# Moving TensorE's operands to whole kilobytes of a partition

## The chip, the cores and the metric

The kernel runs on one core of a Trainium2 chip. The metric is the device time of one execution in microseconds. A profile of one execution is read beside it: it gives the start and duration of each instruction on TensorE (PE for the matmuls, PEld for the loads of their stationary operand), VectorE (DVE), ScalarE (ACT), GpSimd (POOL), and the DMA transfers that SyncE (SP) issues.

## The reference

A decoder trunk of two layers over 256 tokens of width 2048. Layer 0 mixes tokens with 8 stick-breaking heads and 8 dilated-window heads, layer 1 with 16 forgetting-attention heads; each layer then has a gated MLP of inner width 5632 with a depthwise convolution of width 3, and a gated per-layer embedding:

```python
def reference(x, p, positions, ...):
    h = x
    for i in range(DEPTH):
        a = rmsnorm(h, attn_norm[i])
        if i % 2 == 0:
            h = h + sb_dilated_mixer(a, positions, w_in_even[i // 2], w_out_even[i // 2])
        else:
            h = h + fox_mixer(a, w_in_odd[i // 2], b_forget[i // 2], w_out_odd[i // 2])
        h = h + conv_ffn(rmsnorm(h, ffn_norm[i]), w_up[i], conv_w[i], conv_b[i], w_down[i])
        gate = jax.nn.sigmoid(rmsnorm(h, ple_norm[i]) @ w_ple_gate[i])
        h = h + gate * (p[i] @ w_ple[i])
    return rmsnorm(h, final_norm)
```

Everything is float32. Nearly all of the arithmetic is products of a 256-row activation with a weight matrix.

## The kernel before, in words

Activations lie transposed: the 2048 features are 16 tiles (`KT`) of 128 partitions, the 256 tokens run along the free dimension. A float32 product is made from three one-pass products of type float32r. Each operand is kept as two parts, a rounded value and the rest, and `PARTS` (line 194) lists which parts are multiplied: high by high, high by low, low by high.

The activations are in two buffers, `act0` and `act1` (line 114), which a layer uses in turn. One holds, for each of 16 feature tiles, the high part and the low part, 256 float32r each: 1 KB, 1 KB, and so on, 32 KB of each partition. `pact` (line 115) is the same for the per-layer input.

The weights come from memory in one stream in the order in which they are used (`UNITS`). `issue_group` loads up to 2048 columns into one of three `wr` buffers. `split_unit` (lines 158 to 168) makes the two parts of a unit, mostly four feature tiles by 256 output columns: ScalarE casts the high part into a `w` buffer (line 165), VectorE subtracts for the low part (line 166). There are four `w` buffers of 8 KB, and `unit` keeps three units split ahead of use.

`gemm_unit` (line 196) uses a unit in 24 matmuls at line 203. The stationary operand is 128 columns of `w` (512 bytes of each partition), the moving operand is one part of one feature tile of the activation, 256 columns, 1 KB. `gemm_v` (line 229) turns this round: at line 237 the activation is stationary and 256 columns of `w` are moving. `gemm_vf` (line 242) does so for 272 columns once. Each matmul is preceded by its own load of weights.

The program is written in one order; each engine takes its instructions in that order. The head-by-head work of the mixers is put off by a count of units (`defer`, `tick`), so that it falls between the units of the next products. There, score and attention matmuls take full float32 operands; the profile has two records for such a matmul, its two passes. The stick-breaking sums (lines 450 to 455) are again float32r, one pass, up to 512 columns wide.

Scratch tiles of 2 KB come from the tag `t2`, of which there are seven buffers. It serves the squares of the norms (`sq`), the two halves of an MLP group (`yg`, `yv`), the gate (`gt`) and some small tables.

Where a buffer lies within a partition follows from the order in which the pools are opened and the tiles are made. Ahead of all pools lie 16 KB that are set aside and 128 bytes of constants. So in the kernel before `h` begins 128 bytes past a whole kilobyte, and so does everything of whole kilobytes behind it; small tables in `cpool` then shift the weight pool, which begins 192 bytes past one.

Of the kernel before, what the change touches and what calls it, by code (L numbers as in the profile page):

```python
# [10 lines left out]
F32 = mybir.dt.float32  # L11
F32R = mybir.dt.float32r
# [5 lines left out]
P = 128  # L18
D = 2048
S = 256  # L20
# [5 lines left out]
KT = D // P  # L26
# [78 lines left out]
def trunk(ctx: ExitStack, tc: tile.TileContext, xT, pT, pos, gains, conv, bf, cst, wst, out):  # L105
    nc = tc.nc

    cpool = ctx.enter_context(tc.tile_pool(name="cpool", bufs=1))
    wpool = ctx.enter_context(tc.tile_pool(name="wpool", bufs=1))
    work = ctx.enter_context(tc.tile_pool(name="work", bufs=1))  # L110
    psum = ctx.enter_context(tc.tile_pool(name="psum", bufs=1, space=bass.MemoryType.PSUM))

    h = cpool.tile([P, KT, S], F32, name="h")
    bufs = [cpool.tile([P, KT, 2, S], F32R, name=f"act{i}") for i in range(2)]
    pact = cpool.tile([P, 2, 2, S], F32R, name="pact")
    pl = cpool.tile([P, KT, S], F32, name="pl")
    gn = cpool.tile([P, 7, KT], F32, name="gn")
    cv = cpool.tile([P, DEPTH, 2 * FT, 4], F32, name="cv")
# [13 lines left out]
        return psum.tile([P, 2, 512], F32, name=name, tag="at", bufs=2)  # L132

    def t2_tile(name, shape=(P, 2, S), dt=F32):
        return work.tile(list(shape), dt, name=name, tag="t2", bufs=7)

    def t3_tile(name, shape=(P, 768), dt=F32):
        return work.tile(list(shape), dt, name=name, tag="t3", bufs=4)
# [136 lines left out]
    def norm_squares(op):  # L275
        hs = h[:, 2 * op:2 * op + 2, :]
        if op == 0:
            nc.scalar.activation(out=acc, in_=hs, func=AF.Square)
        else:
            sq = t2_tile("sq")  # L280
            nc.scalar.activation(out=sq, in_=hs, func=AF.Square)
            nc.vector.tensor_add(out=acc, in0=acc, in1=sq)
# [26 lines left out]
    def norm_rows(mixer):  # L309

        dg = t2_tile("nd", (P, 2, P))
        ps = at_tile("rps")
        for t in range(2):
            nc.vector.tensor_scalar_mul(out=dg[:, t, :], in0=ident, scalar1=rT[:, t:t + 1])
            if mixer is None:
                nc.tensor.matmul(ps[:, 0, t * P:(t + 1) * P], lhsT=ones, rhs=dg[:, t, :],
                                 start=t == 0, stop=True, skip_group_check=True)
        if mixer is None:
            return ps[:, 0, :S]
        dh, dl = t2_tile("ndh", (P, 2, P), F32R), t2_tile("ndl", (P, 2, P), F32R)  # L320
        nc.scalar.copy(out=dh, in_=dg)
        nc.vector.tensor_sub(out=dl, in0=dg, in1=dh.bitcast(F32))
        for i, x in enumerate((dh, dl)):
            nc.tensor.matmul(ps[:, 0, :S], lhsT=trir[:, 0, :], rhs=x, start=i == 0, stop=i == 1)
        nc.vector.tensor_copy(out=rb, in_=ps[:, 0, :S])
        if mixer:
            nc.vector.tensor_scalar_mul(out=rq, in0=rb, scalar1=SCALE)
# [490 lines left out]
```

## Time and profile before

| what | value |
|---|---|
| time, three runs | 2437.23 us median (2437.09 to 2437.77) |
| the profiled execution | 2438.14 us, of which its span is 2436.3 us |
| granted TensorE clock, mean over the span | 0.997 |
| PE busy | 2414.1 us, 99% of the span, 20990 matmul records |
| DVE busy | 1595.7 us, 65% |
| ACT busy | 1228.3 us, 50% |
| DMA | 458.06 MB, mean 188 GB/s |

The profile's durations of matmuls overlap, since a matmul begins while the one before it drains. The pace of TensorE is therefore read from starts: the time that a row of the chain of waits gives for so many matmuls, divided by their number. The chain of waits is the chain of work that ended last, in order of time. A group's row gives, behind the bar, the busy time of the group in us and the mean duration of one instruction in ns.

### The profile page before, as it was taken

What the parts mean: (1) busy time and instruction counts of PE and PEld (TensorE: products, weight loads), DVE (VectorE), ACT (ScalarE), POOL (GpSimd) and SP (SyncE); (2) the same over time, 40 slices, a digit from 0 to 9 for tenths busy, and PEclk for the clock granted to TensorE, in tenths of its full rate; (3) what the DMA queues carried; (4) which work ended last, traced back from release to release, by engine and by line L of the source; (5) the groups of instructions that cost most, each with busy time, mean ns of one, the idle gap of its engine ahead of it and who ended that gap; (6) DMA issues with size and microseconds to landing.
All of it is one profiled execution on the core that took longest, in us unless ns stands there. A gap on an engine that the chain in (4) does not pass through costs nothing.

```text
span 2436.3 us, 48002 instructions
## 1 busy us (share of the span) xinstructions
PE 2414.1 (99%) x20990; PEld 2400.5 (99%) x20990; DVE 1595.7 (65%) x2157; ACT 1228.3 (50%) x1548; POOL 2.5 (0%) x8
## 2 busy tenths in 40 slices
PE   8999999999999999999999999999999999999997
PEld 8999999999999999999999999999999999999997
DVE  7557666776567657767765555677765776567676
ACT  6554455555355445555554444555543554455553
POOL 0000000000000000000000000000000000000000
PEclk9999999999999999999999999999999999999998
DMA  7444445555555555555554444555555555555553
GB/s 268 169 177 173 169 177 191 194 197 198 190 191 192 188 208 190 191 185 203 187 184 170 165 169 165 190 191 192 195 198 194 191 192 189 203 195 186 189 198 120
DMA packets 66483, 458.06 MB, mean 188 GB/s; under 512 B 7408, under 2 KB 7424, under 8 KB 16608
## 3 DMA queue, kind: packets, MB, share of 16 engines
q1 hardware_dynamic: 66096, 454.53, 52.8%
q8 instruction: 164, 2.69, 0.4%
q0 software_dynamic: 176, 0.46, 0.1%
q14 instruction: 47, 0.39, 0.0%
HBM read 452.86 MB, written 2.10 MB: 187 GB/s over the span
## 4 chain that ended last, share of the span: by engine, by line
PE 97%; DVE 1%; DMA 1%; ACT 1%; issue 0%; SPq 0%; DVEq 0%; ACTq 0%
PE psu L203 39%; PE psd L203 20%; PE pso L203 7%; PE psk L203 7%; PE psv L237 7%; PE psq L203 7%; PE psg L203 7%; DMA wr<-in_w 1%; PE avp L520 1%; PE psp L203 0%; PE pse L716 0%; PE scs L469 0%; PE psv L250 0%; PE sps L511 0%; PE avp L522 0%; PE scs L467 0%
## 5 line engine op out<-in xcount | busy, mean ns | idle before, releaser
L166 DVE TENSOR_TENSOR w<-wr,w 128x1024 fp32r<-128x1024 f32 (+2 forms) x882 | 1051.4, 1193 | 701.2 <-ACT w L165 695.5
L165 ACT CAST w<-wr 128x1024 fp32r<-128x1024 f32 (+2 forms) x882 | 905.6, 1028 | 1082.5 <-PE psu L203 355.1
L203 PE MATMUL psu<-act,w 128*128 128x256 f32 x8448 | 959.3, 276 | 0.0
L203 PEld LDWEIGHTS psu<-act,w 128*128 128x128 f32 x8448 | 958.3, 188 | 0.0
L203 PE MATMUL psd<-act,w 128*128 128x256 f32 x4224 | 479.7, 276 | 0.0
L203 PEld LDWEIGHTS psd<-act,w 128*128 128x128 f32 x4224 | 479.2, 188 | 0.0
L203 PE MATMUL psq<-act,w 128*128 128x256 f32 x1536 | 185.2, 279 | 1.2 <-DVE w L166 1.0
L203 PEld LDWEIGHTS psq<-act,w 128*128 128x128 f32 x1536 | 179.8, 188 | 2.1 <-DVE w L166 1.5
L203 PE MATMUL psk<-act,w 128*128 128x256 f32 x1536 | 180.0, 277 | 0.0
L203 PEld LDWEIGHTS psk<-act,w 128*128 128x128 f32 x1536 | 176.7, 188 | 0.0
L203 PE MATMUL pso<-act,w 128*128 128x256 f32 x1536 | 175.8, 277 | 0.0
L203 PEld LDWEIGHTS pso<-act,w 128*128 128x128 f32 x1536 | 174.9, 188 | 0.0
L237 PE MATMUL psv<-w,act 128*128 128x256 f32 x1440 | 172.7, 279 | 0.0
L237 PEld LDWEIGHTS psv<-w,act 128*128 128x128 f32 x1440 | 168.4, 188 | 1.1
L203 PE MATMUL psg<-act,w 128*128 128x256 f32 x1440 | 164.4, 276 | 0.0
L203 PEld LDWEIGHTS psg<-act,w 128*128 128x128 f32 x1440 | 163.7, 188 | 0.0
L616 DVE TENSOR_TENSOR u<-psu,rb 128x512 f32<-128x512 f32 x88 | 60.8, 691 | 33.3 <-PE psu L203 33.2
L622 DVE SCALAR_TENSOR_TENSOR yg<-u,cv,yg 128x256 f32<-128x256 f32 x176 | 73.3, 477 | 0.0
L622 DVE SCALAR_TENSOR_TENSOR yv<-u,cv,yv 128x256 f32<-128x256 f32 x176 | 73.3, 477 | 0.0
L619 ACT ACTIVATE yg<-u,cv 128x256 f32<-128x256 f32 x88 | 48.0, 594 | 1.0 <-DVE u L616 1.0
L619 ACT ACTIVATE yv<-u,cv 128x256 f32<-128x256 f32 x88 | 48.0, 593 | 0.0
L261 ACT CAST act<-yg 128x512 fp32r<-128x512 f32 x44 | 27.3, 621 | 39.1 <-DVE yg L632 39.1
(173 smaller groups left out, 886.5 us busy)
## 6 DMA issues: line engine op xcount, KB each, us to landing
wr<-in_w SPq DMA_DIRECT2D x388, 1024.0 KB, 4.8
wr<-in_w SPq DMA_DIRECT2D x36, 768.0 KB, 4.3
wr<-in_w SPq DMA_DIRECT2D x8, 896.0 KB, 4.6
wr<-in_w SPq DMA_DIRECT2D x7, 512.0 KB, 6.9
h<-in_x SPq DMA_DIRECT2D x4, 512.0 KB, 7.1
out_dram<-h SPq DMA_DIRECT2D x8, 256.0 KB, 2.4
wr<-in_w SPq DMA_DIRECT2D x2, 816.0 KB, 4.6
ct<-in_c SPq DMA_DIRECT2D x1, 841.0 KB, 6.6
```

The lines of the kernel that those rows point to most:

```text
L165: nc.scalar.copy(out=w[:, :, 0, :], in_=raw)
L166: nc.vector.tensor_sub(out=w[:, :, 1, :], in0=raw, in1=w[:, :, 0, :].bitcast(F32))
L203: nc.tensor.matmul(ps[:, j, :], lhsT=w[:, k, s, js], rhs=act[:, k0 - koff + k, t, :], start=first and j + k + n == 0, stop=last and k == k ...
L237: nc.tensor.matmul(ps[:, t], lhsT=act[:, 4 * i + k, a, tsl], rhs=w[:, k, b], start=i + t + k + n == 0, stop=i == 3 and k == kc - 1 and n = ...
L261: nc.scalar.copy(out=dst[:, :, 0, :], in_=src)
L520: nc.tensor.matmul(av[:, 0, j * S:(j + 1) * S], lhsT=v[:, 0, js], rhs=w[:, j * S:(j + 1) * S], start=j == 0, stop=False, skip_group_check= ...
L616: nc.vector.tensor_mul(out=u[:, :, 2:], in0=ps, in1=rb2)
L619: nc.scalar.activation(out=y[:, j, :], in_=u[:, j, 2:], func=AF.Identity, bias=cv[:, l, t, 3:4], scale=cv[:, l, t, 2:3])
L622: nc.vector.scalar_tensor_tensor(out=y[:, j, :], in0=u[:, j, tap:tap + S], scalar=cv[:, l, t, tap:tap + 1], in1=y[:, j, :], op0=ALU.mult, ...
```

## The change

Two pools are opened first, `apool` and then `wpool`. `apool` begins with a tile `head` of 224 float32 that nothing uses; it fills 896 bytes, so that with the constants ahead of it a whole kilobyte is full. Behind it come `act0`, `act1` and `pact`, then the weight buffers; `h`, the tables and the scratch follow. To make room, the tag `t2` has six buffers rather than seven.

```diff
+    apool = ctx.enter_context(tc.tile_pool(name="apool", bufs=1))
+    wpool = ctx.enter_context(tc.tile_pool(name="wpool", bufs=1))
     cpool = ctx.enter_context(tc.tile_pool(name="cpool", bufs=1))
-    wpool = ctx.enter_context(tc.tile_pool(name="wpool", bufs=1))
...
+    apool.tile([P, 224], F32, name="head")
+    bufs = [apool.tile([P, KT, 2, S], F32R, name=f"act{i}") for i in range(2)]
+    pact = apool.tile([P, 2, 2, S], F32R, name="pact")
     h = cpool.tile([P, KT, S], F32, name="h")
-    bufs = [cpool.tile([P, KT, 2, S], F32R, name=f"act{i}") for i in range(2)]
-    pact = cpool.tile([P, 2, 2, S], F32R, name="pact")
...
     def t2_tile(name, shape=(P, 2, S), dt=F32):
-        return work.tile(list(shape), dt, name=name, tag="t2", bufs=7)
+        return work.tile(list(shape), dt, name=name, tag="t2", bufs=6)
```

Where the operands begin, in the two built programs:

| buffer | before | after |
|---|---|---|
| `act0`, `act1`, `pact` | 128 bytes past a KB | at a KB |
| `wr`, `w` | 192 bytes past a KB | at a KB |
| 1 KB moving operand, line 203 | bytes 128 to 1152: crosses one KB boundary | bytes 0 to 1024: crosses none |
| 1 KB moving operand, line 237 | bytes 192 to 1216: crosses one | bytes 0 to 1024: crosses none |
| 512-byte stationary operand, line 203 | 192 to 704, or 704 to 1216, which crosses | 0 to 512, or 512 to 1024: none crosses |
| 272-column moving operand (1088 bytes), line 250 | crosses one | crosses one |
| 512-column moving operand, line 450 | from 288: crosses two | from 160: crosses two |

No engine's instructions change their order. Of waits, those that a buffer fewer of `t2` brings are new. The place where one stands on a compute engine is the first norm, where ScalarE squares `h` into seven scratch tiles `sq` between its casts of weights (line 165 before, 168 after). Before:

```order
L281 ACTIVATE sq<-h 128x512 x2
L165 CAST w<-wr 128x4x256 [waits DMAHW5_49,DVE_49]
L281 ACTIVATE sq<-h 128x512 x2
L165 CAST w<-wr 128x4x256 [waits DMAHW6_49,DVE_49]
L281 ACTIVATE sq<-h 128x512 x3
L165 CAST w<-wr 128x4x256 [waits DMAHW7_49,DVE_49,PE_49]
```

With the change:

```order
L284 ACTIVATE sq<-h 128x512 x2
L168 CAST w<-wr 128x4x256 [waits DMAHW5_49,DVE_49]
L284 ACTIVATE sq<-h 128x512 x2
L168 CAST w<-wr 128x4x256 [waits DMAHW6_49,DVE_49]
L284 ACTIVATE sq<-h 128x512 x2
L284 ACTIVATE sq<-h 128x512 [waits DVE_49]
L168 CAST w<-wr 128x4x256 [waits DMAHW7_49,PE_49]
```

The seventh square now waits on VectorE, which must first have added the first square to `acc`; the cast behind it no longer needs a wait on VectorE of its own. The other new wait is one of the load of `pr` for layer 1, on SP's queue, on a matmul of the first norm.

## The prediction

> **What bounds the kernel now.** I read the page first, for the engine that never rests, then the chain of waits in order of time, for the pace of that engine.
>
> ```profile
> PE 2414.1 (99%) x20990; PEld 2400.5 (99%) x20990; DVE 1595.7 (65%) x2157; ACT 1228.3 (50%) x1548; POOL 2.5 (0%) x8
> PE 97%; DVE 1%; DMA 1%; ACT 1%; issue 0%; SPq 0%; DVEq 0%; ACTq 0%
> ```
>
> TensorE is 97% of the chain that ended last, so the time is a number of matmuls times the pace at which they start, plus little. The chain of waits gives the pace:
>
> ```profile
> 60.20 8.48 PE psq L203 x72
> 194.89 8.16 PE psv L237 x72
> 420.21 160.50 PE psu L203 x1416
> 580.71 87.04 PE psd L203 x768
> 1212.64 6.73 PE psv L250 x54
> ```
>
> In the MLP, 160.50 us for 1416 matmuls is 113.35 ns from start to start, 87.04 for 768 is 113.33. With the operands' roles turned round (line 237), 8.16/72 is 113.3 as well. I call this the clean pace. In some stretches of layer 0's mixer the same matmul starts every 8.48/72 = 117.8 ns: a second, slower pace, mostly behind full-float32 score matmuls. The 272-column ones start every 6.73/54 = 124.6 ns.
>
> Is 113.3 a wait on somebody? These are four stretches of 1.36 us in the MLP; the columns are each engine's busy time with its instructions, then granted clock, DMA share and GB/s:
>
> ```profile
> 667.75:669.11 1.36, 1.36 (x15) 1.36 (x14) 0.92 (x2) 1.05 (x1) 0.00 (x0) 1.00 0.72 301
> 669.11:670.47 1.36, 1.36 (x15) 1.36 (x14) 0.99 (x1) 0.00 (x0) 0.00 (x0) 1.00 0.00 0
> 670.47:671.83 1.36, 1.36 (x15) 1.36 (x14) 0.23 (x1) 1.05 (x1) 0.00 (x0) 1.00 0.71 96
> 671.83:673.19 1.36, 1.36 (x15) 1.36 (x14) 0.99 (x1) 0.00 (x0) 0.00 (x0) 1.00 0.88 373
> ```
>
> TensorE makes as many starts with no byte of DMA moving and ScalarE idle as at 373 GB/s, at full clock. So the pace is TensorE's own, and no other engine has to be made faster.
>
> **What a stream costs by itself.** The change can only act on the pace, so I ask what 113.3 consists of. Durations by form, full float32 first (two passes, each taking two steps per column), then the one-pass sums of line 450 to 452:
>
> ```profile
> L520 PE MATMUL avp<-s,v 128*128 128x256 f32 x48 | 14.3, 379 | 0.0
> L522 PE MATMUL avp<-s,v 128*128 128x128 f32 x48 | 9.2, 274 | 0.0
> L450 PE MATMUL sps<-el,trir 128*128 128x512 f32 x4 | 1.6, 392 | 0.0
> L452 PE MATMUL sps<-el,trir 128*128 128x256 f32 x4 | 1.1, 280 | 0.0
> ```
>
> In full float32, 128 more columns, which are 256 more steps, cost 379 - 274 = 105 ns. In one pass, 256 more columns, also 256 steps, cost 392 - 280 = 112. Each KB read in one pass thus pays 7 ns that the half-rate stream does not show. That is about what separates 113.3 from the bare 105: the clean pace is the bare steps plus one such charge, with hardly anything fixed on top.
>
> What is the charge tied to? The 1 KB operands cross one KB boundary, the 512-column operand, from byte 288, crosses two, the 272-column one crosses one. Against the slow pace, which the 272 columns share (they follow no clean one), 124.6 - 117.8 = 6.8 ns for 16 columns; bare steps would be 16/256 of 105 = 6.6. So 272 columns pay one charge like 256, and 512 pay two. **Reading one: 7 ns for each KB boundary crossed.** Reading two, 7 ns per KB streamed wherever it lies, would want 7.0 for the 16 columns, and 6.73/54 is too coarse to tell 0.2 ns; but "256 and 272 pay the same, 512 twice" is how boundaries count. I lean to reading one, about two to one.
>
> **The change part by part.** *The moving operands.* After the change none of the 256-column streams crosses a boundary; those of lines 250 and 450 cross as before. The matmuls concerned:
>
> ```profile
> L203 PE MATMUL psu<-act,w 128*128 128x256 f32 x8448 | 959.3, 276 | 0.0
> L203 PE MATMUL psd<-act,w 128*128 128x256 f32 x4224 | 479.7, 276 | 0.0
> L203 PE MATMUL psq<-act,w 128*128 128x256 f32 x1536 | 185.2, 279 | 1.2 <-DVE w L166 1.0
> L203 PE MATMUL psk<-act,w 128*128 128x256 f32 x1536 | 180.0, 277 | 0.0
> L203 PE MATMUL pso<-act,w 128*128 128x256 f32 x1536 | 175.8, 277 | 0.0
> L237 PE MATMUL psv<-w,act 128*128 128x256 f32 x1440 | 172.7, 279 | 0.0
> L203 PE MATMUL psg<-act,w 128*128 128x256 f32 x1440 | 164.4, 276 | 0.0
> L203 PE MATMUL psp<-pact,w 128*128 128x256 f32 x192 | 27.0, 296 | 6.5 <-ACT w L165 6.1 <-DVE w L166 0.5
> L716 PE MATMUL pse<-act,w 128*128 128x256 f32 x96 | 11.0, 276 | 0.0
> ```
>
> Together 8448 + 4224 + 3 x 1536 + 2 x 1440 + 192 + 96 = 20448. The full charge of 7 would bring 113.3 down to 106.3; that is the lower end. The upper end is what TensorE manages where 256 steps and one load of 128 columns repeat and no charge is seen, the 128-column float32 passes:
>
> ```profile
> 75.34 0.38 PE L522 MATMUL avp<-e,v 128*128 128x128 f32 x2
> 75.56 0.60 PE L520 MATMUL avp<-e,v 128*128 128x256 f32 x2
> ```
>
> (75.56 - 75.34)/2 = 110 ns. I take 109, near that row since it is the nearest, a little below since the clean pace showed almost nothing fixed. Saved: 4.33 ns x 20448 = 88.5 us; with 106.3, 143 us; with 110, 68 us; with reading two, nothing. If the charge belongs to lines shorter than a KB, four of 256 bytes say, an aligned stream still crosses three, and a quarter is saved: 1.75 x 20448 = 36 us. The first 35 us, where TensorE waits for weights and `x`, hide about 290 of the matmuls (1.3 us less); the roughly thousand matmuls at the slow pace may save more than 4.3 each (3 us more). I let these two stand against each other.
>
> [...]
>
> *The stationary operands.* Every second dozen of a unit's loads crosses a boundary (704 to 1216), the other does not. Were crossing loads dear on the path, the pace would alternate within 1.36 us; the four stretches above show 15 starts each. I take 0, and 0.2 ns a matmul, 4 us, as the bound.
>
> *The scratch buffer fewer.* The seventh square waits for VectorE's first addition:
>
> ```profile
> 25.99 0.69 DVE L282 TENSOR_TENSOR acc<-acc,sq 128x512 f32<-128x512 f32 x1
> 28.95 1.71 ACT L281 ACTIVATE sq<-h 128x512 f32<-128x512 f32 x3
> ```
>
> The addition is over at 26.68; the third square of the last group begins near 30.1. Cost 0; without these 3.4 us of cover, ScalarE's casts of weights queue behind the square, and TensorE behind them. The wait of `pr` is on a matmul of the first norm, long past when layer 1's input is loaded: 0.
>
> *What must keep up.* From 600 to 1160 us, PE, PEld, DVE and ACT:
>
> ```profile
> 600.00:1160.00 560.00, 560.00 (x4941) 559.90 (x4941) 370.96 (x484) 281.20 (x334) 0.00 (x0) 1.00 0.55 195
> wr<-in_w SPq DMA_DIRECT2D x388, 1024.0 KB, 4.8
> ```
>
> VectorE's 371 us fit in the 539 that 4941 matmuls at 109 ns take. A 1 MB group feeds 48 matmuls, 5.2 us at 109 ns, and lands in 4.8 with two more buffered. Neither becomes the bound.
>
> Sum: the profiled span of 2436.3 becomes 2347.8; that execution took 2438.1, 0.9 over the median, so on the scale of the median 2437.2 - 88.5 = 2349 us.
>
> **The rivals.** *No change.* Reading two, or TensorE is held by the weight loads: PEld is as busy as PE (2400.5), one load per 113.3. For it: exactly one pace whichever operand streams. Against: the float32 passes load 128 columns every 110 ns, and 16 more streamed columns cost 6.8. Time: 2437.
>
> [...]
>
> *A part.* Shorter lines than a KB: 36 us saved, 2401; spread 2385 to 2420.
>
> *Slower: the slow pace everywhere.* The same stream has two stable paces, 113.3 and 117.8, and which it takes depends on how loads and streams fall against each other. Before, a stream and its next load begin 64 bytes apart modulo 512; afterwards they begin on the same byte of a 512-byte block. If that puts every stretch into the slow pattern and the charge stays, the some 19,300 clean ones pay 4.4 ns: +85 us, 2522. It decides as soon as more than the charge returns, 4.4 against 4.3. Against it: before, both paces occur with the same offset (60.20 and 420.21), so the offset alone does not choose between them.
>
> **How the numbers follow.** Boundary charge removed: 0.53, 2349, own range 2330 to 2370. A part: 0.11. No change: 0.24. Slow pace: 0.12. Range 2330 to 2440: it takes in the first three and leaves out the slow pace and the far ends. Faster by over 0.2% (4.9 us, what can be told here from no change): 0.64; the same 0.24; slower 0.12.
>
> **What would show it.** In the chain, the `psu` stretch of 1416 should take 154 to 155 us in place of 160.50, `psd` x768 83.7 in place of 87.04, and the start-to-start of line 237 should fall by as much. The 272-column stretch should stay at 124 to 125, and 512 against 256 columns at 112 ns. PE's busy share stays 99%, DVE's rises to 68%. If `psu` stays at 113.3, the boundary is not what is paid for; at 117.8, the relative offset of load and stream is; at 111 to 112, the lines are shorter.

## The result and the profile after

| | median us | lowest to highest | profiled execution | its span |
|---|---|---|---|---|
| before | 2437.36 | 2437.09 to 2437.77 | 2438.1 | 2436.3 |
| after | 2563.62 | 2562.82 to 2564.78 | 2563.94 | 2562.2 |

The change makes the kernel slower: the ratio is 1.0518, with a 95% interval of 1.0500 to 1.0536. The prediction was 2349 us; its range ended at 2440.

The page of the changed kernel, the busy times and the shares of the chain that ended last:

```profile
PE 2541.0 (99%) x20990; PEld 2528.3 (99%) x20990; DVE 1596.7 (62%) x2157; ACT 1224.3 (48%) x1548; POOL 2.5 (0%) x8
PE 98%; DVE 1%; DMA 1%; ACT 1%; issue 0%; SPq 0%; DVEq 0%; ACTq 0%
```

TensorE has gained 126.9 us of busy time with the same 20990 matmuls, and the span has gained 125.9. VectorE and ScalarE are as busy as before, to about 1 and 4 us. So nothing new is waited for: the starts themselves come further apart. The chain of waits of the changed kernel (start, length, engine, tile, line, matmuls) shows by how much:

```profile
60.18 8.64 PE psq L206 x72
199.66 8.64 PE psv L240 x72
435.02 169.92 PE psu L206 x1416
604.94 92.16 PE psd L206 x768
1273.76 6.76 PE psv L253 x54
```

169.92/1416, 92.16/768 and 8.64/72 are all 120.0 ns. Before, there were two paces, 113.3 in most stretches and 117.8 in some; now there is one, and it is slower than both. The 272-column matmuls of the last row take 6.76/54 = 125.2 ns, about what they took. Each of their moving rows is 1088 bytes long and so begins 64 bytes further past a KB than the one before it, in both kernels: the change does not bring their starts into line.

The seven largest groups of matmuls, which answer to the first seven of the nine rows of before:

```profile
L206 PE MATMUL psu<-act,w 128*128 128x256 f32 x8448 | 1015.5, 283 | 0.0
L206 PE MATMUL psd<-act,w 128*128 128x256 f32 x4224 | 507.9, 283 | 0.0
L206 PE MATMUL psq<-act,w 128*128 128x256 f32 x1536 | 192.2, 284 | 1.0 <-DVE w L169 1.0
L206 PE MATMUL psk<-act,w 128*128 128x256 f32 x1536 | 189.5, 283 | 0.0
L206 PE MATMUL pso<-act,w 128*128 128x256 f32 x1536 | 185.6, 283 | 0.0
L240 PE MATMUL psv<-w,act 128*128 128x256 f32 x1440 | 179.3, 284 | 0.0
L206 PE MATMUL psg<-act,w 128*128 128x256 f32 x1440 | 173.9, 283 | 0.0
```

Their busy times rise by 56.2, 28.2, 7.0, 9.5, 9.8, 6.6 and 9.5, together 126.8 us. That is nearly the whole of the 126.9. For each matmul `psq` and `psv` rise least, 4.6 ns against 6.2 to 6.7 in the others, since many of theirs ran at 117.8 before (their mean was 279 ns where `psu` had 276).

### The profile page after: what moved, and what is told of

It is laid out like the page before. It is cut to its first block, busy times and chain, and to the rows that moved or that the text cites. A ratio compares the mean times of both kernels' runs of the same rounds, so it can differ in the third digit from the quotient of the medians.

```text
span 2562.2 us, 48001 instructions
## 1 busy us (share of the span) xinstructions
PE 2541.0 (99%) x20990; PEld 2528.3 (99%) x20990; DVE 1596.7 (62%) x2157; ACT 1224.3 (48%) x1548; POOL 2.5 (0%) x8
## 4 chain that ended last, share of the span: by engine, by line
PE 98%; DVE 1%; DMA 1%; ACT 1%; issue 0%; SPq 0%; DVEq 0%; ACTq 0%
PE psu L206 40%; PE psd L206 20%; PE pso L206 7%; PE psk L206 7%; PE psv L240 7%; PE psq L206 7%; PE psg L206 7%; DMA wr<-in_w 1%; PE avp L523 1%; PE pse L719 0%; PE psp L206 0%; PE scs L472 0%; PE psv L253 0%; PE sps L514 0%; PE avp L525 0%; PE scs L470 0%
## 5 line engine op out<-in xcount | busy, mean ns | idle before, releaser
L206 PE MATMUL psu<-act,w 128*128 128x256 f32 x8448 | 1015.5, 283 | 0.0
L206 PEld LDWEIGHTS psu<-act,w 128*128 128x128 f32 x8448 | 1014.4, 190 | 0.0
L206 PE MATMUL psd<-act,w 128*128 128x256 f32 x4224 | 507.9, 283 | 0.0
L206 PEld LDWEIGHTS psd<-act,w 128*128 128x128 f32 x4224 | 507.3, 190 | 0.0
L206 PE MATMUL psk<-act,w 128*128 128x256 f32 x1536 | 189.5, 283 | 0.0
L206 PE MATMUL pso<-act,w 128*128 128x256 f32 x1536 | 185.6, 283 | 0.0
L206 PEld LDWEIGHTS pso<-act,w 128*128 128x128 f32 x1536 | 184.7, 192 | 0.0
L206 PE MATMUL psg<-act,w 128*128 128x256 f32 x1440 | 173.9, 283 | 0.0
L206 PEld LDWEIGHTS psg<-act,w 128*128 128x128 f32 x1440 | 173.2, 192 | 0.0
L272 ACT ACTIVATE act<-h,gn 128x256 fp32r<-128x256 f32 x96 | 43.5, 502 | 2.1 <-DMA h<-in_x 1.0
```

Of the source, the lines that this page charges most:

```text
L206: nc.tensor.matmul(ps[:, j, :], lhsT=w[:, k, s, js], rhs=act[:, k0 - koff + k, t, :], start=first and j + k + n == 0, stop=last and k == k ...
L272: nc.scalar.activation(out=dst[:, k, 0, :], in_=h[:, k, :], func=AF.Copy, scale=gn[:, g, k:k + 1])
```

## Experiments

The question is which property of the addresses sets the pace. I speak of the **distance**: the first byte of the stationary operand less the first byte of the moving one. In the kernel before it is 192 - 128 = 64 on line 203 and 128 - 192 = -64 on line 237, where the roles are turned round; in the changed kernel it is 0 on both. The theory after the result was that the distance sets the pace; the rival was that the place of each operand in its own KB does. All edits are to the changed kernel. In each, the pace is read from the stretch of 1416 `psu` matmuls and from a stretch of 72 with the roles turned round.

**Old offsets in the new pools, and one common start away from the KB.** The first kernel has the distance and the offsets of before, in the new order of pools and with the buffer fewer. The second keeps the distance 0, but every 1 KB moving operand crosses a KB boundary again.

```diff
 # old offsets: act at 128, w at 192
-    apool.tile([P, 224], F32, name="head")
+    wpool.tile([P, 16], F32, name="gap")
```

> The change as it is, with its order of pools and its six scratch buffers, but the activations at 128 bytes past a KB and the weights at 192, as in the kernel before. Theory D (the pace is set by the distance between where the moving and the stationary operand start): distance 64 as before, line 206 at 113.3 ns, 2437 us. Theory K (a moving operand that starts on a KB boundary is slow): 113.3 ns, 2437 us as well. Theory O (the order of the buffers, or the scratch buffer fewer, is what costs): 120 ns, 2563 us.

```diff
 # both at 128
-    apool.tile([P, 224], F32, name="head")
```

> Activations and weights both at 128 bytes past a KB: every moving operand crosses a KB boundary and none starts on one, but both operands start on the same byte modulo 512. Theory D: 120 ns as with the change, 2563 us. Theory K: 113.3 ns, 2437 us.

**Distance 64 at the KB.** The moving operands of line 206 stay at a KB, and the weights move by 64 bytes.

```diff
+    wpool.tile([P, 16], F32, name="gap")
```

> Activations at a whole KB as with the change, weights 64 bytes past one: the moving operands of line 206 start on a KB and cross none, distance 64. Theory D: 113.3 ns, 2437 us. Theory K: line 206 stays at 120 ns, about 2555 us, and only line 240, whose moving operand is the weights, goes back to 113.3. The prediction's charge per boundary crossed, freed of the distance: line 206 at 107 to 110 ns, 2350 to 2370 us, line 240 at 113.3.

**Distance 32.**

```diff
+    wpool.tile([P, 8], F32, name="gap")
```

> Activations at a whole KB, weights 32 bytes past one. Theory D: a pace of its own for a distance of 32; if blocks of 64 bytes are what the two operands share, the pace of distance 0, 120 ns and 2563 us; if finer, between 113.3 and 120. Theory K: 120 ns at line 206, 113.3 at line 240, about 2555 us.

With both operands at 128 the time is 2564.45 us, in its chain:

```profile
435.20 169.91 PE psu L205 x1416
199.85 8.64 PE psv L239 x72
```

With the weights 64 bytes behind a KB it is 2442.94 us:

```profile
418.34 160.51 PE psu L207 x1416
193.47 8.16 PE psv L241 x72
1137.33 76.32 PE psg L207 x648
2348.73 65.01 PE psg L207 x552
```

These two settle where the operands lie. A stream that crosses a boundary at distance 0 takes 120.0 ns; a stream that crosses none at distance 64 takes 113.4, as before the change. The boundary has no price; the distance has. The last two rows tell of the 5.5 us that separate this run from the kernel before (2437.45 beside it): `psg` ran at 76.32/648 = 117.8 ns, and so in layer 1, where before it ran at the clean pace (73.46 and 62.58 us). That is 5.3 us more. Up to the MLP this kernel is not behind but 1.9 us ahead (418.34 against 420.21), so the order of the pools and the missing scratch buffer cost nothing that can be seen.

The kernel with the old offsets took 2498.25 us in one execution and 2442.28 in another. The chain of the first:

```profile
330.29 73.46 PE pso L206 x648
403.75 8.17 PE psu L206 x72
418.23 166.77 PE psu L206 x1416
```

The same distance thus has two paces, 73.46/648 = 113.4 and 166.77/1416 = 117.8, as the trace of before had shown on a small scale. The clock does not tell the two executions apart: 0.998 was granted in the slower, 0.997 in the faster. I come back to it below. At distance 32 the time is 2530.09 us:

```profile
429.82 167.56 PE psu L207 x1416
197.91 8.41 PE psv L241 x72
```

118.3 ns at +32, and 8.41/72 = 116.8 at -32. So the pace does not depend on the size of the distance alone: its sign counts, or else the role of the operand. These two are not told apart, since +32 is seen on line 207 alone and -32 on line 241 alone.

**The rest of the circle.** If the distance counts modulo 128, then 96 is like -32 and 128 like 0; modulo 256, only 256 is like 0; modulo 512, 256 isn't like 0 either.

```diff
 # 24, 32, 48 and 64 float32: 96, 128, 192 and 256 bytes
+    wpool.tile([P, 24], F32, name="gap")
```

> Weights 96 bytes past a KB, activations at a KB: distance +96 at line 206's matmuls, -96 at line 240's. Theory P128 (the pace repeats with every 128 bytes of distance): +96 acts as -32, whose pace the weights at 32 showed in line 240's place (8.40/72 = 116.6 ns), and -96 as +32 (118.3): about 2500 us. Theory P512 (the operands only get in each other's way when near, so that farther is better): under 113.3 ns, under 2437 us.

> Weights 128 bytes past a KB: distance 128. Theory P128: as distance 0, 120 ns at both lines, 2564 us. Theory P512: under 113.3 ns, 2320 to 2430 us.

> Weights 192 bytes past a KB: distance 192. Theory P128: as distance 64, that is 113.3 ns, or 117.8 in the stretches that fall into the second pace: 2437 to 2500 us. Theory P512: under 113.3 ns, 2320 to 2430 us.

> Weights 256 bytes past a KB: distance 256, the farthest in a block of 512. Theory P128: 120 ns, 2564 us. Theory P512: the fastest of all, near 109 ns, about 2350 us. If the pace repeats with 256 bytes, 120 ns here and new paces at 96, 128 and 192.

They took 2521.07, 2538.07, 2511.65 and 2563.79 us. Their chains, one fence for each:

```profile
339.13 76.90 PE pso L207 x648
430.99 166.15 PE psu L207 x1416
197.73 8.64 PE psv L241 x72
```

```profile
431.32 168.02 PE psu L207 x1416
198.22 8.54 PE psv L241 x72
```

```profile
59.90 8.16 PE psq L207 x72
423.45 166.77 PE psu L207 x1416
194.69 8.17 PE psv L241 x72
230.96 8.48 PE psv L241 x72
```

```profile
434.83 169.91 PE psu L207 x1416
199.47 8.64 PE psv L241 x72
```

At 256 bytes everything is as at 0: 120.0 in both. At 128 it is not (118.7), so neither 128 nor 512 is the period. That 256 is one rests on this pair, and on 192 and -64, which share the 113.3. With 256 as the period, the paces line up like this (ns from start to start, from the rows above):

| distance | pace | read on |
|---|---|---|
| 0, 256 | 120.0 | both roles, every stretch shown |
| 32 | 118.3 | line 207 |
| 64 | 113.4 or 117.8 | both roles |
| 96 | 117.3 or 118.7 | line 207 |
| 128 | 118.7 | both roles |
| 160 (-96) | 120.0 | line 241 |
| 192 (-64) | 113.3 or 117.8 | line 207; 113.3 on line 241 |
| 224 (-32) | 116.8 | line 241 |

64 and 192 have the lowest pace of these, and 192 is -64, so that in the layout of before one line has the one and the other line the other. Each kernel of these experiments but the first had one execution up to here, and a pace that was seen need not be the only one at its distance: 96 has two as well, 76.90/648 = 118.7 in `pso` beside the 117.3.

**Between the tried steps.** A smaller shift, by starting the matrix inside a slightly longer slot:

```diff
 # 12 or 20 float32: 48 or 80 bytes
-        w = wpool.tile([P, 2048], F32R, name="w", tag="w", bufs=4)
-        w = w[:, :2 * kc * cw].rearrange("p (k s c) -> p k s c", s=2, c=cw)
+        w = wpool.tile([P, 2112], F32R, name="w", tag="w", bufs=4)
+        w = w[:, 12:12 + 2 * kc * cw].rearrange("p (k s c) -> p k s c", s=2, c=cw)
```

> Activations at a KB, weights 48 bytes past (modulo 256), between 32 (118.3 ns) and 64 (113.3 or 117.8). Theory L with a smooth dependence: 114 to 118 ns, 2450 to 2510 us. If only multiples of 64 can fall into step: 117 to 119 ns, 2510 to 2540 us. If the best distance lies beside 64: under 113.3 ns, under 2437 us.

> Weights 80 bytes past, between 64 and 96 (117.3 ns). The same three cases as at 48: 114 to 117 ns; 117 to 118 ns; under 113.3 ns.

2532.93 and 2538.83 us. The chain at 48 bytes:

```profile
341.00 79.91 PE pso L206 x648
436.18 166.77 PE psu L206 x1416
1688.61 167.56 PE psu L206 x1416
```

And at 80:

```profile
431.35 168.03 PE psu L206 x1416
```

166.77/1416 is 117.8, 167.56/1416 in layer 1 is 118.3, and 79.91/648 is 123.3, slower than at distance 0: three paces at one distance. At 80 bytes the `psu` stretch ran at 118.7 ns. The times are nearest the second case, but neither 123.3 nor 118.7 lies in its bounds. At these two distances no pace under 113.3 is hidden; others between the steps were not tried.

**Whose reads make the difference?** One kernel lets each weight load at line 206 read a single column 128 times, so that it stays on the same 4 bytes of a partition rather than going through 512, at distance 0 and at 64.

```diff
-                    nc.tensor.matmul(ps[:, j, :], lhsT=w[:, k, s, js], rhs=act[:, k0 - koff + k, t, :],
+                    one = w[:, k, s, j * P:j * P + 1].to_broadcast([P, P])
+                    nc.tensor.matmul(ps[:, j, :], lhsT=one, rhs=act[:, k0 - koff + k, t, :],
```

> The change, distance 0, but at line 206 the stationary operand is one column of the weights taken 128 times (step 0), so that a load reads 4 bytes of a partition rather than 512; each product is thus that of one weight column, and the result is not the reference's. Theory L (the load's reads of memory collide with the stream's, at a rate set by the distance): without them the pace leaves 120 ns for under 113.3, down to 107 to 110, near 2320 us. Theory O (the stream, not the load, pays, by where it starts): 120 ns, 2560 us. If the one column collides with the stream whenever that passes it: over 113.3, at both distances alike.

> The same at distance 64. Theory L: the same pace as at distance 0, since there is no sweep of the load left that could be in or out of step. Theory O: 113.3 ns, or 117.8, 2440 to 2510 us.

The times are 2452.38 at distance 0 and 2435.8 at 64. The chain at 0:

```profile
194.33 8.64 PE psv L241 x72
333.15 75.60 PE pso L207 x648
408.76 8.40 PE psu L207 x72
423.60 160.50 PE psu L207 x1416
```

And at 64:

```profile
328.83 73.45 PE pso L208 x648
416.81 160.48 PE psu L208 x1416
```

At distance 0, line 241, whose loads are unchanged, stays at 120.0. The edited line goes from 120.0 to 160.50/1416 = 113.3 in the MLP and to 75.60/648 = 116.7 in `pso`, though its streams begin where they did. So it is not the stream alone that pays for its start: which addresses the load reads makes the difference between 120.0 and less. What ScalarE and VectorE write is the same in both kernels, so it is not their writes that cost. Theory L has the direction, but not the size: it asked for less than 113.3, and 113.3, with streams that begin at a KB and a load that stays on one column, is again the lowest pace, as low as in any run here. It also asked for the same pace at both distances, and `pso` differs: 116.7 at 0, 113.4 at 64. At distance 0 this kernel has two paces too. The 116.7 goes on into the first `psu` stretch, 8.40/72, and behind the small matmuls of the norm the pace is 113.3. Why `pso` takes the slower one is open.

**Does a load that covers more bytes do better or worse?** With the two halves of the weights interleaved, a load takes its 128 columns in steps of 8 bytes, and covers 1 KB.

```diff
-        w = w[:, :2 * kc * cw].rearrange("p (k s c) -> p k s c", s=2, c=cw)
+        w = w[:, :2 * kc * cw].rearrange("p (k c s) -> p k s c", s=2, c=cw)
```

with no gap and with gaps of 64, 128 and 192 bytes:

> The split weights lie with high and low part side by side, column by column, so that a stationary operand is 128 columns in steps of 8 bytes, 1 KB rather than 512 bytes; activations and weights both at a KB, distance 0. [...] Theory M (the cost is in the first bytes alone, where both start): 120 ns as before at distance 0. Theory C (steps of 8 bytes cost the load twice the reads): over 120 ns, over 2600 us, at every distance.

> The same at distance 64. [...] Theory M: 113.3 or 117.8 ns, 2437 to 2512 us. Theory C: over 120 ns.

> The same at distance 128, half of the 256 bytes with which the pace repeats. [...] Theory M: 118.7 ns, 2538 us. Theory C: over 120 ns.

> The same at distance 192. [...] Theory M: 113.3 or 117.8 ns. Theory C: over 120 ns.

The times are 2732.78, 2732.86, 2754.24 and 2736.83 us. Three chains show where the time goes, at 0, 64 and 128 bytes:

```profile
240.97 16.55 PE psv L240 x72
518.53 169.92 PE psu L206 x1416
```

```profile
241.20 16.56 PE psv L241 x72
518.84 169.92 PE psu L207 x1416
```

```profile
427.73 77.77 PE pso L207 x648
520.73 171.49 PE psu L207 x1416
```

Most of the added time is line 240, where the interleaved weights are the moving operand: 16.55/72 = 229.9 ns, twice the clean pace. Where they are the stationary operand, the pace is 120.0 at 0, at 64 and at 192 (169.92 us too), and at 128 it is 171.49/1416 = 121.1 in `psu` and 77.77/648 = 120.0 in `pso`. With such a load none of the four distances reaches the clean pace. So theory M, by which the load's first bytes decide, falls: the distances 64 and 192 do not help. Theory C wanted over 120 at every distance, and only 128 shows that, by 1.1 ns; its time of over 2600 us came true by line 240, not by the loads. Against the dense load the interleaved one costs nothing at 0, and at 64 it costs 6.6 ns over the faster of the two paces there. What it is in such a load that keeps the pace at 120.0 or above is not settled by these four.

**How stable is distance 64?** The two layouts with that distance again, each executed several times beside the kernel before:

> Offsets 128 and 192 in the new order of buffers, once more and timed. If chance chooses, times spread between 2442 and 2500 us as in its two executions so far; if those two were an accident of one chip, 2442 us each time.

> Distance 64 with the activations at a KB, once more and timed: line 207's pace at distance 64 was seen at 113.3 and, with the old offsets in the new order of buffers, at 117.8 for whole layers. If chance at each entry into a stream chooses, times between 2440 and 2525 us; if the layout chooses, 2443 us each time.

| | times us | ratio (95% interval) |
|---|---|---|
| before, beside them | 2436.88 to 2437.92, 7 executions | |
| old offsets in the new pools | 2469.71, 2498.21, 2498.33, 2498.88, 2499.12 | 1.0252 (1.0234 to 1.0269) |
| weights at 64 | 2497.93, 2498.57, 2498.89, 2499.1 | 1.0251 (1.0236 to 1.0266) |

The execution of 2469.71 us was profiled. Its chain, layer 0 and layer 1:

```profile
403.13 8.17 PE psu L206 x72
417.61 166.78 PE psu L206 x1416
1656.92 160.51 PE psu L206 x1416
```

Layer 0's MLP ran at 117.8, layer 1's at 113.4, on the same addresses. An MLP of one layer has 8448/2 + 4224/2 = 6336 matmuls; 6336 x 4.43 = 28 us. Hence the three times of one and the same kernel, 28 us apart: about 2442 with both layers at the faster pace, 2470 with one, 2498 with none. The first row, ahead of the norm's small matmuls, is at 113.4, the second behind them at 117.8, and the pace then holds to the end of the MLP. Between the two rows, 48 `psu` matmuls take 5.57 us in layer 0 (from 411.63) and 5.57 in layer 1 (from 1650.95), so the layers still agree there; they part with the next row. So the choice falls where the long stretch is entered. The kernel before came out at 2436.9 to 2438.1 in every execution timed here, so its entry always fell right; why that of the two others mostly did not, with the same distance, was not found.

## Why the prediction was wrong

- **TensorE sets the time.** Right. VectorE, the DMA groups and the scratch buffer cost nothing that can be seen, as worked out; all 126 us are pace.
- **"Reading one: 7 ns for each KB boundary crossed."** This is the step that failed, and the forecast of 88.5 us hung on it. Streams that cross none run at 113.4 (weights at 64) and streams that cross one at 120.0 (both at 128). Nothing is paid at the boundary, and no run came below 113.3. That leaves, for the 113.3, what the rival of no change named: reading two, a charge that goes with the streaming itself, or the weight loads, one for each 113.3 ns. No run here tells these two apart. Reading two was put at one to two against, by counting boundaries on rows that, as the text said, could not tell 0.2 ns. The 7 ns were no firmer. They are what is left if a full-float32 column counts as exactly two one-pass steps; that was the author's estimate, and the trace of before shows 215 ns from start to start for a full-float32 pass of 256 columns (two passes from 74.91 to 75.34 us) against 113.3 in one pass, 1.9 times. The 112 among them is a difference of means of four matmuls each, and in the changed kernel, whose 512-column stream crosses two boundaries as before, the same two groups (lines 453 and 455, `el`) give 390 - 282 = 108 ns in place of 112.
- **"The stationary operands. [...] I take 0".** Failed as well. The question asked there, whether the load's own boundary is paid for, was answered rightly by the even pace. But the load counts through its distance from the stream, which the even pace could not show: on line 203 every load has the same distance modulo 256.
- **The slower rival** had the cause, the same start of load and stream, and three errors. Its block of 512 bytes is one of 256 (256 gives 120.0 like 0). Its price, the slow pace of 117.8, was too small: 120.0 is a pace of its own that no stretch of before shows, and by it the rival's 19,300 matmuls pay 6.67 ns, 129 us, close to the 126 measured. And its chance, 0.12, was lowered by an argument that does not hold: "both paces occur with the same offset (60.20 and 420.21), so the offset alone does not choose between them". That is true of 64, where two paces are possible, and says nothing of 0, where each stretch shows one.
- **The signs** were of use. "At 117.8, the relative offset of load and stream is" named the suspect, and the first four runs confirmed it.

## What to carry to other kernels

TensorE loads one operand while it streams the other (PEld was busy for 2528.3 us of the changed kernel, PE for 2541.0), so ask of an address not only how it lies in itself but how it lies against the other operand; here shifting one pool of the changed kernel by 32 to 128 bytes moved the time by 1 to 5% with not one instruction changed. A trace of one layout holds one or two values of such a variable and can't price another: several readings that fit it are a reason to widen the range on both sides, and a gap of a few float32 ahead of a pool is a cheap experiment. Where a layout has two stable paces, time it in several executions, since one alone (2442.94 us here) may show the rarer.

## What was not expected of the hardware

- The pace of a one-pass 256-column matmul depends on the distance of its two operands' starts, alike at 0 and 256 bytes: 120.0 ns at 0, 113.4 or 117.8 at 64 and 192, and 116.8 to 120.0 at the other steps of 32; 123.3 was seen at 48.
- At 64 two paces are stable over thousands of matmuls, and one kernel has three times, 28 us apart. More than one pace was seen at 48 and 96 too, but none besides 120.0 at 0 with the full load.
- A moving operand in steps of 8 bytes takes 229.9 ns at distance 0, where a dense one takes 113.3 to 123.3 at the distances tried. ScalarE's casts that write in such steps are dearer too, at distance 0, by the page's mean: 1117 ns against 1023.

The casts' rows, changed kernel first:

```profile
L168 ACT CAST w<-wr 128x1024 fp32r<-128x1024 f32 (+2 forms) x882 | 901.7, 1023 | 1225.9 <-PE psu L206 404.6
```

```profile
L168 ACT CAST w<-wr 128x1024 fp32r<-128x1024 f32 (+2 forms) x882 | 984.5, 1117 | 1285.0 <-PE psu L206 379.5
```
